# Gate and value products as three 256-column matmuls per weight tile, accumulated in one half of a PSUM bank

## The chip, the core and the metric

The kernel runs on one core of a Trainium2 chip. The metric is the time of one execution on the device, in microseconds (us). The kernel before the change takes 951.92 us (the median of two runs, 951.59 and 952.25 us).

A core has engines that run side by side. TensorE (PE in the profile) multiplies matrices. It holds one operand, the weights, in its array and streams the other through it, and it writes sums into PSUM. The profile keeps the loading of weights apart, as PEld. VectorE (DVE) and ScalarE (ACT) do elementwise work, GpSimd (POOL) and SyncE (SP) mostly issue transfers. SBUF is the working memory with 128 partitions. PSUM has eight banks of 512 fp32 numbers in each partition.

## The reference

One encoder layer for 256 positions and a width of 2048, in fp32: a norm, one input projection, windowed attention and a Fourier mix, an output projection with a residual, and then a feed-forward block, which is what the change touches:

```python
up = h @ w_up                                  # (256 x 2048) @ (2048 x 11008)
gate, val = up[..., :D_FF], up[..., D_FF:]     # D_FF = 5504
gate = conv(gate, dw_w) + dw_b                 # width 3, along the positions, per channel
act = gelu(gate) * val
x = x + act @ w_down                           # (256 x 5504) @ (5504 x 2048)
```

The result is normed once more and returned.

## The kernel before

**Products in two parts.** TensorE multiplies fp32 numbers in a rounded form here (type `float32r`), which alone is not exact enough. So each operand is split into a high part, rounded to that type, and a low part, which is what the rounding left over. A product is high times high, plus high times low, plus low times high. For a weight tile, `split_parts` does this: a ScalarE copy makes the high part `hi` (line 170), a VectorE subtraction the low part `lo` (line 171). Both lie in one buffer `parts` of 2 x 2048 + 128 numbers per partition, of which there are three in turn. `parts_tile` sets how far each part is moved inside its buffer. The table `PLACES` has these offsets, in numbers of 4 bytes: (0, 16) for "still" weights, (28, 28) for the blocks of the down-projection.

**A gate or value unit.** The up-projection is cut into 43 tiles of 128 gate channels and 43 of 128 value channels. Each of these 86 units takes a weight block of 1 MB, 128 columns of `w_up` in 16 k tiles of 128 rows. In `still_weights` the weights are what stands in the array. The moving operand is the normed input, which was put into the tiles `hT` (named hU for this stage) with the high part of the 256 positions in columns 0 to 255 and their low part in columns 256 to 511. For each k tile there are two matmuls:

```python
nc.tensor.matmul(ps, hi[:, s], h, ...)                       # line 326, 512 columns
nc.tensor.matmul(ps[:, 0:S], lo[:, s], h[:, 0:S], ...)       # line 328, 256 columns
```

The first fills a whole PSUM bank: hi times high on the left, hi times low on the right. The second adds lo times high on the left. The two halves have to be added afterwards. `scaled_sum` does that: ScalarE copies the right half to SBUF (line 810), VectorE adds the left half to it (line 812), and VectorE multiplies the sum with the norm's scale `r2b` (line 813). Then `gate_conv` and `gate_gelu`, or `val_mult`, make the activations.

**Order of the work.** The program order on each engine is written by hand. `items` is the list of all units: 16 gate and value units, then four groups in which the remaining ones alternate with products of the down-projection (`by_parts`, lines 1019 to 1021, all matmuls of 512 columns), then the last gate and value units among the last parts of the down-projection (`moving_weights`, lines 309 to 311). `ff_step(n)` runs after the matmuls of item n: it first issues what was noted under `beside` for this item (`scaled_sum` of the item before, and the convolution of the one before that), then splits the weights of item n + 2 (`split_item`), and then what was noted under `behind`. SyncE loads a raw weight block three units ahead (`load`). The first two units of the stage (gate and value of tile 0) are run together, because the last quarter of their moving operand comes late. The third one keeps its low parts back by four k tiles (`lag=4`).

The same `still_weights` makes the queries and keys earlier on, with a lag of four in each of 16 units. There the last five low parts stand one behind the other. Three small stages work with matmuls of 256 columns alone and have the same three products of parts: `fourier_rows` (line 491), `scores` (line 602) and `values` (line 674).

Of the kernel before, what the change touches and what calls it, by code (L numbers as in the profile page):

```python
# [8 lines left out]
F32 = mybir.dt.float32  # L9
F32R = mybir.dt.float32r  # L10
AF = mybir.ActivationFunctionType
ALU = mybir.AluOpType

P = 128
D = 2048
S = 256
NK = D // P
# [46 lines left out]
def ff_items():  # L64


    def ups(tiles):
        return [(kind, j) for j in tiles for kind in ("gate", "val")]

    items = ups(range(8))  # L70
    for g in range(N_GROUPS):
        todo = {
            "u": ups(range(8 * g + 8, 8 * g + 16)),
            "s": [("product", g, c, p) for c in range(2) for p in PRODUCTS[c]],
        }
        items += [todo[c].pop(0) for c in PATTERN]
        assert not any(todo.values())
    items += [("down", 0, c) for c in range(4)] + ups(LAST)
    items += [("down", 1, c) for c in range(4)] + [("last", c) for c in range(4)]
    return items  # L80
# [3 lines left out]
def block_kernel(  # L84
# [18 lines left out]
    nc = tc.nc  # L103
# [10 lines left out]
    def bank(pool, name):  # L114
        return pool.tile([P, 512], F32, tag=pool.name, name=name)


    units = [(w_in[i], 2048, "first" if i < N_QK else "still") for i in range(24)]
    units += [(w_out[i], 2048, "moving") for i in range(16)]
    n_front = len(units)  # L120
    items, up_index = ff_items(), {}
    for n, it in enumerate(items):
        if it[0] == "product":
            continue
        up_index[n] = len(units)
        if it[0] in ("gate", "val"):
            units.append((w_up[2 * it[1] + (it[0] == "val")], 2048, "still"))
        elif it[0] == "down":
            units.append((w_down_late[4 * it[1] + it[2]], 2048, "moving"))
        else:  # L130
            units.append((w_down_last[it[1]], 512 * len(LAST), "moving"))
    RAW = 3
    raws, halves = {}, {}


    PLACES = {"still": (0, 16), "first": (16, 16), "moving": (0, 0), "product": (28, 28)}

    def parts_tile(name, place):
        t = wp.tile([P, 2 * 2048 + 128], F32R, tag="parts", name=name, bufs=3)
        oh, ol = PLACES[place]  # L140
        return t[:, oh : oh + 2048], t[:, 2048 + ol : 4096 + ol]

    def load(i, pieces=1):
        if i < len(units) and i not in raws:
# [37 lines left out]
    hT = []  # L182
# [70 lines left out]
    ps = bank(dn, "ps_warm")  # L253
# [61 lines left out]
    def still_weights(hi, lo, ps, kk, lag=0):  # L315


        todo = [("hi", k) for k in kk[: lag + 1]]
        for n, k in enumerate(kk):
            todo.append(("lo", k))  # L320
            todo += [("hi", q) for q in kk[lag + 1 + n : lag + 2 + n]]
        for part, k in todo:
            h = hT[k // 4][:, k % 4, :]
            s = slice(k * P, (k + 1) * P)
            if part == "hi":
                nc.tensor.matmul(ps, hi[:, s], h, start=k == 0, stop=False)  # L326
            else:
                nc.tensor.matmul(  # L328
                    ps[:, 0:S], lo[:, s], h[:, 0:S], start=False, stop=k == NK - 1
                )  # L330

    def hk(k):
# [15 lines left out]
    before, beside, behind = {}, {}, {}  # L348

    def at(when, i, f, *a):  # L350
        when.setdefault(i, []).append((f, a))
# [13 lines left out]
    for c in range(4):  # L365
        t = base.tile([P, 4, 512], F32R, tag=f"hT{c}", name=f"hT{c}")
        hT.append(t)
    ps_u = [bank(mm, f"ps_u{b}") for b in range(2)]
    for k in range(NK):
# [5 lines left out]
        hi, lo = halves[c]  # L375
# [392 lines left out]
    for n, (c, kq) in enumerate(OUT_ORDER):  # L768
# [15 lines left out]
        if kq >= 2:  # L784
            part = "a" if kq == 2 else "f"
            ps = ps_a[c] if kq < 3 else ps_a[c, "f"]
# [15 lines left out]
    fp = ctx.enter_context(tc.tile_pool(name="fp", bufs=2))  # L802
    hT[:] = hT2
    r2b = fp.tile([P, S], F32, tag="r2b", name="r2b", bufs=1)
    parts = {}
    gate_out, sums_of, act = {}, {}, {}

    def scaled_sum(ps, name):
        tmp = fp.tile([P, S], F32, tag="ftmp", name=f"ft_{name}")
        nc.scalar.activation(tmp, ps[:, S : 2 * S], AF.Copy)  # L810
        add = fp.tile([P, S], F32, tag="fadd", name=f"fa_{name}", bufs=3)
        nc.vector.tensor_tensor(add, ps[:, 0:S], tmp, ALU.add)
        nc.vector.tensor_tensor(add, add, r2b, ALU.mult)
        sums_of[name] = add
# [85 lines left out]
    def ring_load():  # L900
        if ring_next[0] < len(ring):
            key = ring[ring_next[0]]
            ring_next[0] += 1
            ring_tiles[key] = fp.tile([P, 2048], F32, tag="rawd", name="rawd%d%d%s" % key)
            nc.sync.dma_start(ring_tiles[key], weights_of(*key))
# [20 lines left out]
    def first_sums(g, c):  # L926

        a, b = ring_tiles[g, c, "a"], ring_tiles[g, c, "b"]
        x = ring_tiles["x"] = fp.tile([P, 2048], F32, tag="sumw", name=f"sumw{g}{c}", bufs=1)
        nc.vector.tensor_tensor(x, a, b, ALU.add)  # L930
        nc.gpsimd.dma_start(b, weights_of(g, c, "d"), accum_op=ALU.add)
# [14 lines left out]
    def ff_step(n):  # L946
        todo, later[:] = list(later), []
        for f in todo:
            next(f, None)
        run(beside, n)  # L950
        split_item(n + 2)
        for f in todo:
            for _ in f:
                pass
        run(behind, n)

    def up_posts(n, kind, j, ps):
        if kind == "gate":
            at(beside, n + 1, scaled_sum, ps, f"g{j}")
            at(beside, n + 2, gate_conv, j)  # L960
            at(behind, n + 2, gate_gelu, j)
        else:
            at(beside, n + 1, scaled_sum, ps, f"v{j}")
            at(beside, n + 2, val_mult, j)
            if j % 8 == 7 and j < 8 * N_GROUPS:
                g = j // 8
                at(behind, n + 1, operand, g, "P1")
                at(behind, n + 2, operand, g, "N4")
                at(behind, n + 3, operand_sums, g, 0)
                at(behind, n + 4, operand, g, "P7")  # L970
                at(behind, n + 4, operand, g, "P2")
                at(behind, n + 5, operand_sums, g, 1)
                at(behind, n + 5, operand, g, "N5")
                at(behind, n + 6, operand, g, "N3")
                at(behind, n + 7, operand, g, "P6")
            if j >= 8 * N_GROUPS:
                at(behind, n + 2, act_parts, j)
# [37 lines left out]
    def by_parts(ps, o, hi, lo, first, last):  # L1015

        for p in range(4):
            s = slice(p * 512, (p + 1) * 512)
            nc.tensor.matmul(ps, o[:, 0, p, :], hi[:, s], start=first and p == 0, stop=False)  # L1019
            nc.tensor.matmul(ps, o[:, 1, p, :], hi[:, s], start=False, stop=False)  # L1020
            nc.tensor.matmul(ps, o[:, 0, p, :], lo[:, s], start=False, stop=last and p == 3)  # L1021
# [58 lines left out]
    for q in range(2):  # L1080
        kind, j = items[q]
        ps = bank(mm, f"ps_{kind}{j}")
# [10 lines left out]
    spread(rstd_of(tot2, D, "2"), r2b, "2")  # L1093
    ff_step(1)
    up_posts(1, *items[0], pair[0][0])
    up_posts(2, *items[1], pair[1][0])

    for n, it in enumerate(items):
        if n < 2:
            continue  # L1100
        if it[0] == "last":
            break
        if n in (8, 9):
            ring_load()
        if n == 13:
            pending.append(lambda: first_sums(0, 0))
        if it[0] in ("gate", "val"):
            kind, j = it
            ps = bank(mm, f"ps_{kind}{j}")
            still_weights(*halves.pop(up_index[n]), ps, range(NK), lag=4 if n == 2 else 0)  # L1110
            ff_step(n)
            up_posts(n, kind, j, ps)
            continue
        if it[0] == "product":
            kind, g, c, p = it
            end = g == N_GROUPS - 1
            if (c, p) in held:
                by_parts(held[c, p], parts[p], *halves.pop(it), g == 0, end)
            else:
                ps = bank(mm, f"ps_{p}{g}{c}")  # L1120
                by_parts(ps, parts[p], *halves.pop(it), True, True)
                at(beside, n + 1, product_out, g, c, p, ps)
            if end and p == "N4":
                at(behind, n + 1, shared_out, c)
        else:
            kind, g, c = it
            hi, lo = halves.pop(up_index[n])
            ps = [bank(mm, f"ps_l{g}{c}{b}") for b in range(2)]
            for b in range(2):
                moving_weights(hi, lo, 512, LATE[g], act.get, b, ps[b], True, True)  # L1130
            at(beside, n + 1, down_out, c, ps)
            if (g, c) == (0, 0):
                gfb = fp.tile([P, D], F32, tag="sumw", name="gfb", bufs=1)
                nc.gpsimd.dma_start(gfb, normf_g.partition_broadcast(P))
        ff_step(n)
# [149 lines left out]
```

## Time and profile before

| | |
|---|---|
| median of the runs | 951.92 us |
| the profiled execution | 953.02 us |
| its span in the profile | 951.2 us |
| TensorE matmuls | 5089, busy 940.7 us |
| weight loads | 5089, busy 813.0 us |
| VectorE | busy 744.8 us |
| ScalarE | busy 540.3 us |

The span runs from the first to the last instruction, and some 1.8 us of the execution lie around it. The time of one matmul in the profile is longer than its distance to the next, because the next one starts while the one before still drains. So the distances from start to start, which the view of instructions in order of time gives, say what a matmul costs, and not its own duration. The duration of a weight load is to be read in the same way.

### The profile page before, as it was taken

How to read it: one execution, taken by the hardware profiler on the slowest of the kernel's cores; microseconds unless marked ns; L12 is line 12 of the kernel's file. 1: busy time of each engine (PE TensorE's matmuls, PEld its weight loads, DVE VectorE, ACT ScalarE, POOL GpSimd, SP SyncE). 2: the span in 40 equal slices, each digit the busy share in tenths (PEclk: the TensorE clock that was granted, in tenths of full speed). 3: DMA queues.
4: the chain of work that ended last, by engine and by line, in shares of the span. 5: the costliest groups of instructions: out<-in, count | busy, mean ns of one | idle time of the engine just before them, and what ended most of it. 6: DMA issues, size and time to landing. Idle time of an engine off the chain costs nothing.

```text
span 951.2 us, 12801 instructions
## 1 busy us (share of the span) xinstructions
PE 940.7 (99%) x5089; PEld 813.0 (85%) x5089; DVE 744.8 (78%) x924; ACT 540.3 (57%) x654; POOL 44.7 (5%) x59
## 2 busy tenths in 40 slices
PE   8999999999999999999999999999999999999996
PEld 7788999888888888888888888888888888888885
DVE  5667878667676779887898877998889979888774
ACT  5846666544464456655555555565556755653444
POOL 0000000000000000000000000000000000000003
PEclk9999999999999999999999999999999999999999
DMA  8844444445556675978687787777987696765542
GB/s 313 346 180 178 147 164 140 171 177 177 183 177 216 265 240 202 260 254 282 214 271 232 239 291 257 251 238 223 295 253 245 213 294 201 243 241 205 197 133 89
DMA packets 33548, 211.59 MB, mean 222 GB/s; under 512 B 3792, under 2 KB 4304, under 8 KB 9424
## 3 DMA queue, kind: packets, MB, share of 16 engines
q1 hardware_dynamic: 29744, 184.54, 52.1%
q0 software_dynamic: 3600, 26.22, 14.2%
q8 instruction: 40, 0.66, 0.2%
q14 instruction: 20, 0.16, 0.1%
q10 hardware_dynamic: 144, 0.01, 0.0%
HBM read 208.65 MB, written 2.10 MB: 222 GB/s over the span
## 4 chain that ended last, share of the span: by engine, by line
PE 92%; DVE 3%; DMA 2%; issue 1%; ACT 1%; SPq 0%; POOL 0%; ACTq 0%; POOLq 0%
PE ps_val L326 16%; PE ps_gate L326 16%; PE ps_val L328 8%; PE ps_gate L328 8%; PE ps_q L326 5%; PE ps_P L1020 3%; PE ps_P L1021 3%; PE ps_P L1019 3%; PE ps_q L328 2%; PE ps_a L311 2%; PE ps_a L309 2%; PE ps_a L310 2%; PE ps_N L1021 2%; PE ps_N L1020 2%; PE ps_N L1019 2%; DMA raw<-in_w_in 2%
## 5 line engine op out<-in xcount | busy, mean ns | idle before, releaser
L171 DVE TENSOR_TENSOR parts<-raw,parts 128x2048 fp32r<-128x2048 f32 (+3 forms) x145 | 313.1, 2159 | 62.5 <-ACT parts L170 62.5
L170 ACT ACTIVATE parts<-raw 128x2048 fp32r<-128x2048 f32 (+3 forms) x144 | 262.0, 1820 | 72.4 <-PE ps_l L311 25.9
L326 PE MATMUL ps_val<-hU,parts 128*128 128x512 f32 x688 | 236.2, 389 | 0.0
L326 PE MATMUL ps_gate<-hU,parts 128*128 128x512 f32 x688 | 235.8, 389 | 0.0
L328 PE MATMUL ps_val<-hU,parts 128*128 128x256 f32 x688 | 189.9, 276 | 0.0
L328 PE MATMUL ps_gate<-hU,parts 128*128 128x256 f32 x688 | 189.3, 276 | 0.0
L326 PEld LDWEIGHTS ps_val<-hU,parts 128*128 128x128 f32 x688 | 129.2, 188 | 26.6
L326 PEld LDWEIGHTS ps_gate<-hU,parts 128*128 128x128 f32 x688 | 129.1, 188 | 26.7
L328 PEld LDWEIGHTS ps_val<-hU,parts 128*128 128x128 f32 x688 | 129.2, 188 | 1.2 <-DVE parts L171 0.2
L328 PEld LDWEIGHTS ps_gate<-hU,parts 128*128 128x128 f32 x688 | 128.9, 188 | 1.2
L810 ACT ACTIVATE ft_g<-ps_gate 128x256 f32<-128x256 f32 x43 | 16.5, 384 | 116.6 <-PE ps_gate L328 116.6
L810 ACT ACTIVATE ft_v<-ps_val 128x256 f32<-128x256 f32 x43 | 16.5, 384 | 88.3 <-PE ps_val L328 88.3
L326 PE MATMUL ps_q<-hT,parts 128*128 128x512 f32 x192 | 61.3, 393 | 0.0
L1019 PE MATMUL ps_P<-parts_P,op_P 128*128 128x512 f32 x128 | 49.8, 389 | 0.0
L1020 PE MATMUL ps_P<-parts_P,op_P 128*128 128x512 f32 x128 | 49.8, 389 | 0.0
L1021 PE MATMUL ps_P<-parts_P,op_P 128*128 128x512 f32 x128 | 49.8, 389 | 0.0
L328 PE MATMUL ps_q<-hT,parts 128*128 128x256 f32 x192 | 45.5, 278 | 0.0
L916 DVE TENSOR_TENSOR parts_N<-sumw,parts_N 128x2048 fp32r<-128x2048 f32 x16 | 36.6, 2290 | 10.1 <-ACT parts_N L915 10.1
L326 PEld LDWEIGHTS ps_q<-hT,parts 128*128 128x128 f32 x192 | 35.2, 188 | 6.8
L309 PE MATMUL ps_a<-parts,cat 128*128 128x512 f32 x96 | 37.9, 394 | 0.0
L1021 PE MATMUL ps_N<-parts_N,op_N 128*128 128x512 f32 x96 | 37.5, 390 | 0.1
L311 PE MATMUL ps_a<-parts,cat 128*128 128x512 f32 x96 | 37.5, 390 | 0.0
(323 smaller groups left out, 1564.7 us busy)
## 6 DMA issues: line engine op xcount, KB each, us to landing
raw<-in_w_up SPq DMA_DIRECT2D x86, 1024.0 KB, 5.0
raw<-in_w_in SPq DMA_DIRECT2D x21, 1024.0 KB, 4.9
raw<-in_w_out SPq DMA_DIRECT2D x16, 1024.0 KB, 4.8
sumw<-in_w_down POOLq DMA_DIRECT2D x16, 1024.0 KB, 8.4
raw<-in_w_down_late SPq DMA_DIRECT2D x8, 1024.0 KB, 4.8
raw<-in_w_down_last SPq DMA_DIRECT2D x4, 768.0 KB, 4.2
raw<-in_w_in SPq DMA_DIRECT2D x8, 256.0 KB, 6.5
xs<-in_x SPq DMA_DIRECT2D x4, 512.0 KB, 11.1
```

Of the source, the lines that this page charges most:

```text
L170: nc.scalar.activation(hi[:, s], raw[:, s], AF.Copy)
L171: nc.vector.tensor_tensor(lo[:, s], raw[:, s], f32(hi[:, s]), ALU.subtract)
L309: nc.tensor.matmul(ps, ah, wh, start=first and q == q0, stop=False)
L310: nc.tensor.matmul(ps, al, wh, start=False, stop=False)
L311: nc.tensor.matmul(ps, ah, wl, start=False, stop=last and q == q0 + len(kk) - 1)
L326: nc.tensor.matmul(ps, hi[:, s], h, start=k == 0, stop=False)
L328: nc.tensor.matmul(ps[:, 0:S], lo[:, s], h[:, 0:S], start=False, stop=k == NK - 1)
L810: nc.scalar.activation(tmp, ps[:, S : 2 * S], AF.Copy)
L916: nc.vector.tensor_tensor(lo, src, f32(hi), ALU.subtract)
L1019: nc.tensor.matmul(ps, o[:, 0, p, :], hi[:, s], start=first and p == 0, stop=False)
L1020: nc.tensor.matmul(ps, o[:, 1, p, :], hi[:, s], start=False, stop=False)
L1021: nc.tensor.matmul(ps, o[:, 0, p, :], lo[:, s], start=False, stop=last and p == 3)
```

## The change

All gate and value units but the first two, 84 of 86, use a new function `still_thirds` in the place of `still_weights`. It issues three matmuls of 256 columns for each k tile, all of which accumulate into the left half of the bank. For 32 of the 84 units (`apart`) the product with `lo` stands between the two with `hi`. The lag of the third unit is gone. `scaled_sum` then has nothing to add: VectorE multiplies the left half with `r2b` straight out of PSUM, and the copy and the addition are left out. The 84 units also differ in the places of their parts: the first 64 of them go twice through 8 offsets of `hi` and 4 of `lo`, the last 20 have a pair each from a list, and where the offset of `hi` is the larger one, `lo` is put into the first half of the buffer and `hi` into the second.

```diff
-            units.append((w_up[2 * it[1] + (it[0] == "val")], 2048, "still"))
+            units.append((w_up[2 * it[1] + (it[0] == "val")], 2048, "up"))
...
+    def up_place():
+        n = used[0]
+        used[0] += 1
+        if n < 2:
+            return PLACES["still"]
+        n -= 2
+        if n < 64:
+            return 8 * (n % 8), 16 * (n // 8 % 4)
+        n -= 64
+        odd = [(52, 52), (52, 16), (4, 4), (20, 20), (36, 36), (60, 60), (12, 12), (28, 28),
+               (44, 44), (4, 20), (20, 52), (52, 36), (52, 0), (60, 16), (12, 16), (0, 52),
+               (16, 52), (32, 52), (48, 52), (44, 16)]
+        return odd[n]
...
-        oh, ol = PLACES[place]
-        return t[:, oh : oh + 2048], t[:, 2048 + ol : 4096 + ol]
+        oh, ol = up_place() if place == "up" else PLACES[place]
+        if oh <= ol:
+            return t[:, oh : oh + 2048], t[:, 2048 + ol : 4096 + ol]
+        return t[:, 2048 + oh : 4096 + oh], t[:, ol : ol + 2048]
...
+    def still_thirds(hi, lo, ps, apart):
+        for k in range(NK):
+            h = hT[k // 4][:, k % 4, :]
+            s = slice(k * P, (k + 1) * P)
+            todo = [(hi, 0), (hi, S), (lo, 0)]
+            if apart:
+                todo = [(hi, 0), (lo, 0), (hi, S)]
+            for n, (w, o) in enumerate(todo):
+                nc.tensor.matmul(
+                    ps[:, 0:S], w[:, s], h[:, o : o + S],
+                    start=k == 0 and n == 0, stop=k == NK - 1 and n == 2,
+                )
...
-    def scaled_sum(ps, name):
+    def scaled_sum(ps, name, whole=True):
+        if whole:
+            add = fp.tile([P, S], F32, tag="fadd", name=f"fa_{name}", bufs=3)
+            nc.vector.tensor_tensor(add, ps[:, 0:S], r2b, ALU.mult)
+            sums_of[name] = add
+            return
...
-            at(beside, n + 1, scaled_sum, ps, f"g{j}")
+            at(beside, n + 1, scaled_sum, ps, f"g{j}", j > 0)
...
-            still_weights(*halves.pop(up_index[n]), ps, range(NK), lag=4 if n == 2 else 0)
+            still_thirds(*halves.pop(up_index[n]), ps, 4 <= up_index[n] // 8 - n_front // 8 < 8)
```

More of the change, by code (lines that the diff above doesn't have):

```diff
@@ L136, in block_kernel @@
     PLACES = {"still": (0, 16), "first": (16, 16), "moving": (0, 0), "product": (28, 28)}
+    used = [0]
+    def up_place():
[11 more added lines that the diff above has]
+        return odd[n]
     def parts_tile(name, place):
         t = wp.tile([P, 2 * 2048 + 128], F32R, tag="parts", name=name, bufs=3)
-        oh, ol = PLACES[place]
-        return t[:, oh : oh + 2048], t[:, 2048 + ol : 4096 + ol]
+        oh, ol = up_place() if place == "up" else PLACES[place]
+        if oh <= ol:
+            return t[:, oh : oh + 2048], t[:, 2048 + ol : 4096 + ol]
+        return t[:, 2048 + oh : 4096 + oh], t[:, ol : ol + 2048]
     def load(i, pieces=1):
@@ L962, in up_posts @@
         else:
-            at(beside, n + 1, scaled_sum, ps, f"v{j}")
+            at(beside, n + 1, scaled_sum, ps, f"v{j}", j > 0)
             at(beside, n + 2, val_mult, j)
```

## The prediction

> **What bounds the kernel now.** I read the page's head first, then the chain that ended last, then the waits of TensorE, and last the gate and value units in order of time.
>
> ```profile
> span 951.2 us, 12801 instructions
> PE 940.7 (99%) x5089; PEld 813.0 (85%) x5089; DVE 744.8 (78%) x924; ACT 540.3 (57%) x654; POOL 44.7 (5%) x59
> PEclk9999999999999999999999999999999999999999
> ...
> PE 92%; DVE 3%; DMA 2%; issue 1%; ACT 1%; SPq 0%; POOL 0%; ACTq 0%; POOLq 0%
> PE ps_val L326 16%; PE ps_gate L326 16%; PE ps_val L328 8%; PE ps_gate L328 8%; PE ps_q L326 5%; PE ps_P L1020 3%; PE ps_P L1021 3%; PE ps_P L1019 3%; PE ps_q L328 2%; PE ps_a L311 2%; PE ps_a L309 2%; PE ps_a L310 2%; PE ps_N L1021 2%; PE ps_N L1020 2%; PE ps_N L1019 2%; DMA raw<-in_w_in 2%
> ```
>
> 92% of the chain lies on TensorE, and 48% of it in the two lines that the change rewrites. The granted clock is full throughout. So what counts is the distance between one matmul and the next. The waits of weight loads from 272 us to the end, the part that the change touches, leave almost nothing else:
>
> ```profile
> PEld ps_l L309 <- issue: 0.6, 1, 0.6
> PEld ps_N L1021 <- DVE parts_N L916: 0.5, 1, 0.5
> PEld ps_val L328 <- DVE parts L171: 0.2, 1, 0.2
> ```
>
> That is 1.3 us in all. A helper engine that gets faster can give back no more than this.
>
> **The unit as it is.** In order of time, within a gate unit, and the first matmul of a gate unit and of the value unit behind it:
>
> ```profile
> 502.14 0.28 PE L328 MATMUL ps_gate<-hU,parts 128*128 128x256 f32 x1
> 502.25 0.39 PE L326 MATMUL ps_gate<-hU,parts 128*128 128x512 f32 x1
> 502.48 0.28 PE L328 MATMUL ps_gate<-hU,parts 128*128 128x256 f32 x1
> 502.59 0.39 PE L326 MATMUL ps_gate<-hU,parts 128*128 128x512 f32 x1
> ...
> 894.21 0.39 PE L326 MATMUL ps_gate<-hU,parts 128*128 128x512 f32 x1
> ...
> 899.65 0.39 PE L326 MATMUL ps_val<-hU,parts 128*128 128x512 f32 x1
> ```
>
> From start to start the 512-column matmul takes 0.23 us and the 256-column one 0.11. A whole unit takes 899.65 - 894.21 = 5.44 us, so a k tile takes 5.44 / 16 = 0.340 us. The two shapes stand as 2 to 1, so 256 columns cost 0.340 / 3 = 0.113 us here. The streaming rate is therefore the same in both shapes: three matmuls of 256 columns at this rate take 0.340 us again. Nothing is won on TensorE; the question is whether the rate holds.
>
> **What the change does to TensorE.** A k tile gets a third weight load. In the unit as it is, each 256-column matmul, during which the next weights have to come in, is followed by one that lasts twice as long and leaves slack. Afterwards every load has only the time of a 256-column matmul. The trace has stretches of just this kind: `fourier_rows` (one long stretch, here as a piece of the chain), `values` with the same order of high, high, low, and the five low parts at the end of a query unit, each with the start of what follows.
>
> ```profile
> 49.01 2.88 PE ps_f L491 x24
> ...
> 81.71 0.76 PE L328 MATMUL ps_q<-hT,parts 128*128 128x256 f32 x5
> 82.31 0.88 PE L602 MATMUL ps_s<-kT,qT 128*128 128x256 f32 x6
> ...
> 102.25 0.40 PE L674 MATMUL ps_o<-pt,v_hi 128*128 128x256 f32 x2
> 102.48 0.28 PE L674 MATMUL ps_o<-pt,v_lo 128*128 128x256 f32 x1
> 102.60 0.40 PE L674 MATMUL ps_o<-pt,v_hi 128*128 128x256 f32 x2
> 102.84 0.28 PE L674 MATMUL ps_o<-pt,v_lo 128*128 128x256 f32 x1
> 102.96 0.60 PE L652 MATMUL ps_t<-ident,sc 128*128 128x128 f32 x4
> ```
>
> The long stretch takes 2.88 / 24 = 0.120 us per matmul. The five low parts take (82.31 - 81.71) / 5 = 0.120, and the six of `values` (102.96 - 102.25) / 6 = 0.118. None of them reaches 0.113, although their tiles lie in quite different places. The short stretches start with slack from the 512-column matmuls ahead, so the long one is nearest to a unit of 48 matmuls. I take 0.1195 us: nearer to 0.120, with a little taken off because the 84 units have many different places and some may be kinder.
>
> The two `hi` products of a k tile use the same weights, back to back in 52 units. If the second load were left out, two loads per k tile would remain. `values` answers that, since it uses `v_hi` twice running:
>
> ```profile
> L674 PEld LDWEIGHTS ps_o<-pt,v_hi x48: 187/188/192, 95.0 to 191.8; 128*128 128x128 f32 x48
> L674 PE MATMUL ps_o<-pt,v_hi x48: 278/281/285, 95.2 to 191.9; 128*128 128x256 f32 x48
> ```
>
> 48 matmuls with `v_hi`, 48 loads: the same weights are loaded again.
>
> So a k tile takes 3 x 0.1195 = 0.3585 us, 0.0185 more than now. The change covers 84 units x 16 = 1344 k tiles: **+24.9 us**. The order in the 32 units that are `apart` changes neither the number of loads nor the shapes, and I cost it at nothing.
>
> **What it does to VectorE and ScalarE.**
>
> ```profile
> L810 ACT ACTIVATE ft_v<-ps_val 128x256 f32<-128x256 f32 x43 | 16.5, 384 | 88.3 <-PE ps_val L328 88.3
> L812 DVE TENSOR_TENSOR fa_g<-ps_gate,ft_g 128x256 f32<-128x256 f32 x43 | 18.1, 422 | 24.1 <-ACT ft_g L810 24.1
> L813 DVE TENSOR_TENSOR fa_v<-fa_v,r2b 128x256 f32<-128x256 f32 x43 | 18.3, 425 | 1.5
> L915 ACT ACTIVATE parts_N<-sumw 128x2048 fp32r<-128x2048 f32 x16 | 30.6, 1910 | 0.0
> L916 DVE TENSOR_TENSOR parts_N<-sumw,parts_N 128x2048 fp32r<-128x2048 f32 x16 | 36.6, 2290 | 10.1 <-ACT parts_N L915 10.1
> L170 ACT ACTIVATE parts<-raw 128x2048 fp32r<-128x2048 f32 x130 | 248.9, 1915 | 58.7 <-PE ps_l L311 16.8 <-PE ps_a L311 14.2 <-PE ps_ff L311 9.2
> L171 DVE TENSOR_TENSOR parts<-raw,parts 128x2048 fp32r<-128x2048 f32 x130 | 297.4, 2288 | 55.5 <-ACT parts L170 55.5
> ```
>
> 84 copies of 0.384 us go from ScalarE (32 us) and 84 additions of 0.422 us from VectorE (35 us). The multiplication that stays reads PSUM as the addition did, at 0.42 us. All of it runs beside TensorE, which waits 1.3 us for everything together, so I count half of that, **-0.6 us**, as a guess between 0 and -1.3. The new wait, of VectorE for the last matmul of a unit, replaces ScalarE's wait for the same matmul and VectorE's for the copy; behind it in VectorE's queue stands the split of a unit two items ahead, as before, and it now starts earlier by a copy and an addition. The new places cost the two engines nothing that a row shows: the blocks at (28, 28) take 1910 and 2290 ns, those at the other places 1915 and 2288. The dropped lag costs nothing either: the low part of the third unit is written by 265.2 us, and its matmuls start at 272.96:
>
> ```profile
> 262.94 2.29 DVE L171 TENSOR_TENSOR parts<-raw,parts 128x2048 fp32r<-128x2048 f32 x1 [1.20 <-ACT parts L170]
> ...
> 272.96 1.40 PE L326 MATMUL ps_gate<-hU,parts 128*128 128x512 f32 x5
> ```
>
> Transfers keep their number and order on the queues of SP and POOL, and a slower TensorE only gives them more time.
>
> **The sum.** +24.9 - 0.6 = +24.3 us on the profiled execution's 953.0 us gives 977.3. That execution lies 1.1 us above the median of 951.92, so the median should become **976 us**. About 2% of the time, 19 us, is what a measurement of this kernel can tell from no change.
>
> **Rivals.**
>
> *The loads stay hidden (not slower).* The rate of 0.113 us per 256 columns holds in the new units too. For it speaks that a load does fit into 0.113 us in every unit now: at 502.14 the weights of the matmul at 502.25 had to come in while 256 columns streamed. Eight transposes of 128 columns, each with a load, took even less, (265.68 - 264.89) / 8 = 0.10 us:
>
> ```profile
> 264.89 1.04 PE L750 MATMUL ps_x<-ident,xs 128*128 128x128 f32 x8
> 265.68 0.47 PE L326 MATMUL ps_val<-hU,parts 128*128 128x512 f32 x1
> ```
>
> Then the 0.120 of the stretches would come from the places of their tiles, and the places of the 84 units would mostly be kinder. The time would be 951.9 - 0.6 = 951 us, and up to 956 where the mean is 0.1145 (1344 x 0.0035 = 4.7 us more). The forecast gives way to it from a mean of 0.118 downwards: (0.118 x 3 - 0.340) x 1344 = 18.8 us, where the 2% end. Against it speak the three stretches above, none below 0.118. The Trainium skill's page "TensorE: Matmul & The Clock Gate" stands on this rival's side: its section "Back-to-back issue gap" gives N / 2.4 + 2.5 ns from one matmul to the next, and its section "LDWEIGHTS (loading the stationary operand)" gives the number of columns / 1.2 ns for a load. By these, 256 columns take an estimated 109 ns, a load 107 ns and hides, and three thirds (327 ns) against 216 + 109 = 325 ns would cost 1344 x 2 ns = 3 us. The trace does not agree with the page here: 113 and 227 ns in the alternating unit, 120 ns in the long stretch.
>
> *Bad places.* Where the weights lie sets how a load and the stream disturb each other. The same code with the same offsets already shows two rates, here at the start of a query unit's and a later unit's steady part:
>
> ```profile
> 71.34 0.40 PE L326 MATMUL ps_q<-hT,parts 128*128 128x512 f32 x1
> ...
> 74.84 0.40 PE L326 MATMUL ps_q<-hT,parts 128*128 128x512 f32 x1
> ...
> 78.09 0.39 PE L326 MATMUL ps_q<-hT,parts 128*128 128x512 f32 x1
> ...
> 81.49 0.39 PE L326 MATMUL ps_q<-hT,parts 128*128 128x512 f32 x1
> ```
>
> Ten k tiles take 3.50 us in the first and 3.40 in the second, 0.010 us more for each tile, or 0.005 for each load. If most of the new places add that to 0.120, a matmul takes 0.125, a k tile 0.375, and the time rises by 0.035 x 1344 = 47 us to 998 us. Against it: the stretches with other tiles do not come out above 0.120.
>
> *Faster.* A rate below 0.113 per 256 columns would be needed; 19 us are 0.014 us per k tile, that is 0.1085 per matmul. No place in the trace shows 256 columns in less than 0.11.
>
> **Chances.** The forecast, 0.117 to 0.123 us per matmul (+14.8 to +39.0 us, or 966 to 990 us with the 0.6 taken off): 0.70, of which 0.12 lies under the 2%. Hidden loads: 0.17. Bad places: 0.10. Faster: 0.03. That makes slower by over 2% 0.58 + 0.10 = 0.68, within 2% 0.12 + 0.17 = 0.29, faster 0.03. The range runs from 953 us, which takes in the upper half of the hidden loads, to 990 us; it leaves out 0.03, some 0.08 of the hidden loads and 0.07 of the bad places.
>
> **What the profile afterwards would show.** Matmuls should number 5089 + 1344 = 6433, with as many loads. Within a new unit the starts should lie 0.12 us apart and a unit should take 16 x 0.3585 = 5.74 us where it took 5.44, with no engine named as the cause. The groups of line 810 should shrink to two instructions, VectorE should fall by about 35 us and ScalarE by about 32. I would be wrong if the starts lie 0.113 us apart, if units with different places differ by far more than 0.1 us, or if TensorE now waits for a named engine.

## The result and the profile after

The changed kernel takes 975.18 us (median of two runs, 974.71 and 975.65) against 951.92: a ratio of 1.0244, with a 95% interval of 1.0200 to 1.0288. It is slower by 23.3 us.

The head of the page after, its chain, and the new groups (line, engine, operation, tiles, count, then busy time, mean duration in ns, and idle time of the engine before them):

```profile
span 972.6 us, 15315 instructions
PE 962.3 (99%) x6433; PEld 884.6 (91%) x6433; DVE 710.6 (73%) x840; ACT 517.1 (53%) x570; POOL 44.6 (5%) x59
...
PE 94%; DMA 3%; ACT 1%; DVE 0%; issue 0%; POOL 0%; ACTq 0%; POOLq 0%; SPq 0%
...
L360 PEld LDWEIGHTS ps_val<-hU,parts 128*128 128x128 f32 x2016 | 243.8, 188 | 2.4
L360 PE MATMUL ps_val<-hU,parts 128*128 128x256 f32 x2016 | 245.8, 281 | 0.0
L360 PEld LDWEIGHTS ps_gate<-hU,parts 128*128 128x128 f32 x2016 | 242.2, 188 | 2.4
L360 PE MATMUL ps_gate<-hU,parts 128*128 128x256 f32 x2016 | 244.1, 280 | 0.0
...
L844 DVE TENSOR_TENSOR fa_g<-ps_gate,r2b 128x256 f32<-128x256 f32 x42 | 17.7, 422 | 26.7 <-PE ps_gate L360 26.6
```

There are 1344 more matmuls and as many more loads, one for each k tile. TensorE carries 94% of the chain. VectorE is busy 34.2 us less and ScalarE 23.2 us less. Of the waits of weight loads from 272 us to the end, one is left in the place of three:

```profile
PEld ps_l L327 <- issue: 0.3, 1, 0.3
```

So the time did not go to a wait. It went to the distance between matmuls, and the units in order of time show something that no group does (start, duration, instruction; a unit lasts until the next one starts, and the last line of each piece is cut off by the end of the stretch that was asked for):

```profile
295.83 5.61 PE L360 MATMUL ps_gate<-hU,parts 128*128 128x256 f32 x48
301.28 5.82 PE L360 MATMUL ps_val<-hU,parts 128*128 128x256 f32 x48
306.94 5.71 PE L360 MATMUL ps_gate<-hU,parts 128*128 128x256 f32 x48
312.48 5.82 PE L360 MATMUL ps_val<-hU,parts 128*128 128x256 f32 x48
318.14 5.81 PE L360 MATMUL ps_gate<-hU,parts 128*128 128x256 f32 x48
323.79 5.81 PE L360 MATMUL ps_val<-hU,parts 128*128 128x256 f32 x48
329.44 5.91 PE L360 MATMUL ps_gate<-hU,parts 128*128 128x256 f32 x48
335.19 0.99 PE L360 MATMUL ps_val<-hU,parts 128*128 128x256 f32 x7
...
487.04 6.11 PE L360 MATMUL ps_val<-hU,parts 128*128 128x256 f32 x48
492.99 0.40 PE L360 MATMUL ps_gate<-hU,parts 128*128 128x256 f32 x2
```

The same 48 matmuls take 301.28 - 295.83 = 5.45 us in the first unit, whose parts lie at (32, 0), 5.66 in the next, at (40, 0), 335.19 - 329.44 = 5.75 at (16, 16) and 492.99 - 487.04 = 5.95 at (56, 48). The first is within 0.01 us of a unit before the change (5.44).

Added up from the starts of all instructions in the two traces, the 84 units take 19.3 us more than 84 x 5.44, and the matmuls of the blocks of the down-projection between them (`by_parts`) take 2.0 us more (154.7 against 152.7). The two spans differ by 21.4 us. So nearly all of the loss lies inside the units. Only 4 of the 84, at (32, 0) twice, (0, 32) and (32, 32), stay under 5.5 us.

### The profile page after: what moved, and what is told of

Read it like the earlier page. It is cut to its first block, busy times and chain, and to the rows that moved or that the text cites. A ratio compares the mean times of both kernels' runs of the same rounds, so it can differ in the third digit from the quotient of the medians.

```text
span 972.6 us, 15315 instructions
## 1 busy us (share of the span) xinstructions
PE 962.3 (99%) x6433; PEld 884.6 (91%) x6433; DVE 710.6 (73%) x840; ACT 517.1 (53%) x570; POOL 44.6 (5%) x59
## 4 chain that ended last, share of the span: by engine, by line
PE 94%; DMA 3%; ACT 1%; DVE 0%; issue 0%; POOL 0%; ACTq 0%; POOLq 0%; SPq 0%
PE ps_val L360 25%; PE ps_gate L360 24%; PE ps_q L344 5%; PE ps_P L1057 3%; PE ps_P L1059 3%; PE ps_P L1058 3%; DMA raw<-in_w_in 3%; PE ps_N L1058 2%; PE ps_q L346 2%; PE ps_N L1057 2%; PE ps_N L1059 2%; PE ps_a L329 2%; PE ps_a L327 2%; PE ps_a L328 2%; PE ps_l L327 2%; PE ps_k L344 2%
## 5 line engine op out<-in xcount | busy, mean ns | idle before, releaser
L360 PEld LDWEIGHTS ps_val<-hU,parts 128*128 128x128 f32 x2016 | 243.8, 188 | 2.4
L360 PE MATMUL ps_val<-hU,parts 128*128 128x256 f32 x2016 | 245.8, 281 | 0.0
L360 PEld LDWEIGHTS ps_gate<-hU,parts 128*128 128x128 f32 x2016 | 242.2, 188 | 2.4
L360 PE MATMUL ps_gate<-hU,parts 128*128 128x256 f32 x2016 | 244.1, 280 | 0.0
L953 ACT ACTIVATE parts_N<-sumw 128x2048 fp32r<-128x2048 f32 x16 | 30.7, 1918 | 40.0 <-PE ps_val L360 25.7
L344 PEld LDWEIGHTS ps_q<-hT,parts 128*128 128x128 f32 x192 | 35.2, 188 | 6.8
L327 PE MATMUL ps_a<-parts,cat 128*128 128x512 f32 x96 | 37.9, 394 | 0.0
L1058 PE MATMUL ps_N<-parts_N,op_N 128*128 128x512 f32 x96 | 37.7, 393 | 0.0
L1057 PE MATMUL ps_N<-parts_N,op_N 128*128 128x512 f32 x96 | 37.7, 392 | 0.0
L1059 PE MATMUL ps_N<-parts_N,op_N 128*128 128x512 f32 x96 | 37.5, 391 | 0.0
L329 PE MATMUL ps_a<-parts,cat 128*128 128x512 f32 x96 | 37.5, 390 | 0.0
L328 PE MATMUL ps_a<-parts,cat 128*128 128x512 f32 x96 | 37.4, 389 | 0.0
L844 DVE TENSOR_TENSOR fa_g<-ps_gate,r2b 128x256 f32<-128x256 f32 x42 | 17.7, 422 | 26.7 <-PE ps_gate L360 26.6
L346 PEld LDWEIGHTS ps_q<-hT,parts 128*128 128x128 f32 x192 | 33.5, 188 | 1.0
```

What stands on the lines that cost most here:

```text
L327: nc.tensor.matmul(ps, ah, wh, start=first and q == q0, stop=False)
L328: nc.tensor.matmul(ps, al, wh, start=False, stop=False)
L329: nc.tensor.matmul(ps, ah, wl, start=False, stop=last and q == q0 + len(kk) - 1)
L346: nc.tensor.matmul(ps[:, 0:S], lo[:, s], h[:, 0:S], start=False, stop=k == NK - 1)
L360: nc.tensor.matmul(ps[:, 0:S], w[:, s], h[:, o : o + S], start=k == 0 and n == 0, stop=k == NK - 1 and n == 2,)
```

## The experiments

Theory A is that of the prediction: a matmul of 256 columns with its own load needs about 0.12 us wherever things lie, because the loads pace the stream. Theory B: load and stream disturb each other, depending on where the weights lie in memory against the input that streams. Each experiment starts from the changed kernel. A unit's time is the distance between the starts of two units in the trace.

**All units at (32, 0), and all at (16, 16).**

```diff
 def up_place():
+        if n >= 2:
+            return (32, 0)        # the other run: (16, 16)
...
-    still_thirds(..., 4 <= up_index[n] // 8 - n_front // 8 < 8)
+    still_thirds(..., False)
```

> All 84 units at the place (32, 0), order hi, hi, lo, nothing else changed against the changed kernel. Theory A (the loads pace: a matmul of 256 columns with a load of its own needs about 0.12 us wherever the parts lie; the two units at this place in the changed kernel were an accident of their neighbours): units of about 5.7 us, a time of 972 to 978 us. Theory B (the place decides whether load and stream disturb each other; the two units at (32, 0) took 5.45 us, as the old form did): all units at about 5.45 us, a time of 951 to 954 us, no different from before within 0.3%.

> All 84 units at the place (16, 16), order hi, hi, lo. Theory A: as the changed kernel, 974 to 977 us. Theory B: the two units at this place took 5.75 us with a steady 0.120 per matmul; 84 x (5.75 - 5.44) = 26 us over before and about 1 to 2 us for the products between them: 978 to 981 us.

At (32, 0): 954.02 us against 951.94 for the kernel before on the same chip, a ratio of 1.0021 (1.0012 to 1.0031). At (16, 16): 979.34 us, 1.0290 (1.0273 to 1.0307). The chains of the two, in the same stretch:

```profile
305.13 5.44 PE ps_gate L362 x48
310.57 5.44 PE ps_val L362 x48
```

```profile
301.85 5.76 PE ps_val L362 x48
307.61 5.76 PE ps_gate L362 x48
```

The same program, with the parts moved by some numbers, differs by 25 us. Theory A falls: 48 matmuls with 48 loads run at 5.44 / 48 = 0.113 us each where they lie well, the rate of streaming that the prediction named as the floor. At (16, 16) each one takes 0.120, which is just what the prediction had read off the long stretch of the trace before.

**The old form with the new places.**

```diff
-            at(beside, n + 1, scaled_sum, ps, f"g{j}", j > 0)
+            at(beside, n + 1, scaled_sum, ps, f"g{j}", False)
...
-            at(beside, n + 1, scaled_sum, ps, f"v{j}", j > 0)
+            at(beside, n + 1, scaled_sum, ps, f"v{j}", False)
...
-            still_thirds(*halves.pop(up_index[n]), ps, 4 <= up_index[n] // 8 - n_front // 8 < 8)
+            still_weights(*halves.pop(up_index[n]), ps, range(NK), lag=4 if n == 2 else 0)
```

> The old form of a unit (512 and 256 columns, copy and addition of halves) with the 84 places of the changed kernel. Theory A: a load has slack in the long matmul, so the places do not matter: 951 to 953 us, every unit 5.44 us. Theory B: the places disturb here too, but with two loads for a k tile instead of three and slack behind one of them, so less: units between 5.44 and about 5.65 us that differ by place, 954 to 963 us.

967.12 us against 951.94, 1.0157 (1.0137 to 1.0177), which is more than either theory gave. The places alone, with two matmuls for a k tile as before, cost 15 us. Units go from 5.44 us, at (0, 16), (0, 52) and (32, 52), up to 5.66, and most lie at 5.55 to 5.65. (The first one takes 5.72; it is slower than the others in the kernel before too, with 5.57.) The long matmuls are not spared: at other places those of 512 columns took 228 to 235 ns on average in most units, where they had taken 227.

**The input moved.** In the built program the tiles of the input start 24 numbers behind a multiple of 32, and the buffers of the weight parts 8. So at (32, 0) both weight parts lie 16 from the input, counted in lines of 32 numbers, and at (16, 16) they lie at 0. Here 16 numbers stand ahead of the input's tiles and 48 behind them, so that the input alone moves by 16.

```diff
+    pad = base.tile([P, 16], F32, tag="pad0", name="pad0")
+    nc.gpsimd.memset(pad, 0.0)
     for c in range(4):
         t = base.tile([P, 4, 512], F32R, tag=f"hT{c}", name=f"hT{c}")
         hT.append(t)
+    pad = base.tile([P, 48], F32, tag="pad1", name="pad1")
+    nc.gpsimd.memset(pad, 0.0)
```

> The changed kernel with the moving operand's four tiles 16 numbers further on; the weight parts stay where they were against a line of 64 numbers. Theory A: nothing changes, each unit as in the changed kernel. Theory B, with the distance between weights and stream as what counts: the good places move by 16, so that (16, 48), (48, 16), (48, 48) or (16, 16) have units of 5.44 us, and (32, 0), (0, 32) and (32, 32) lose theirs and go to 5.65 to 5.75. Theory C (the place of the weights alone counts): the good places stay at (32, 0), (0, 32), (32, 32). The total says little here: 965 to 982 us by all of them.

977.74 us (1.0269, 1.0248 to 1.0289), which says little, as expected. The units say much. Here are those at (16, 16), (24, 16), (32, 16), (40, 16) and (48, 16), and the start of the next one:

```profile
332.45 5.81 PE L360 MATMUL ps_gate<-hU,parts 128*128 128x256 f32 x48
338.10 5.86 PE L360 MATMUL ps_val<-hU,parts 128*128 128x256 f32 x48
343.80 5.82 PE L360 MATMUL ps_gate<-hU,parts 128*128 128x256 f32 x48
349.46 5.83 PE L360 MATMUL ps_val<-hU,parts 128*128 128x256 f32 x48
355.12 5.61 PE L360 MATMUL ps_gate<-hU,parts 128*128 128x256 f32 x48
360.57 5.82 PE L360 MATMUL ps_val<-hU,parts 128*128 128x256 f32 x48
```

From start to start the one at (16, 16) takes 5.65 us and the one at (48, 16) 360.57 - 355.12 = 5.45; they had taken 5.75 and 5.70. Each of these places was used once in the order high, high, low and once in the order high, low, high. The two times of each kernel, in us, are those of the two orders, first high, high, low:

```
place       changed kernel    input moved by 16
(32, 0)     5.45  5.45        5.72  5.71
(0, 32)     5.44  5.71        5.67  5.69
(32, 32)    5.44  5.65        5.74  5.76
(16, 16)    5.75  5.75        5.65  5.65
(48, 16)    5.70  5.68        5.45  5.46
(16, 48)    5.71  5.72        5.47  5.70
(48, 48)    5.70  5.70        5.65  5.44
(0, 0)      5.74  5.65        5.84  5.69
(56, 48)    5.94  5.95        5.71  5.72
(8, 0)      5.66  5.65        5.95  5.92
```

The table turns over. What was best at (32, 0) is now best at (48, 16), and what was worst at (56, 48) is now worst at (8, 0), which is (56, 48) moved by 16, counted in lines of 64. The whole grid moves so: of 62 pairs of units in the same order whose two offsets differ by 16 (without the first unit of the stage), 50 agree within 0.03 us, while units at unchanged offsets agree in 21 of 62. What counts is the distance between weights and stream and not the place of the weights alone, which was theory C. That two units at one place can differ by 0.2 us is taken up below.

One pair does not fit a rule in lines of 32. At (0, 0) both parts lie 16 from the input too, and with the input moved they do so at (16, 16). None of these four units is fast (5.74 and 5.65, 5.65 and 5.65; the first of them is the first unit of the stage). So 16 in lines of 32 names the good places found here, but it is not shown to be enough.

**The new form alone, at the place of before.** All units at (0, 16), in the order high, high, low.

> The new form alone: all 84 units with three thirds, order hi, hi, lo, all at (0, 16), the place that every unit had before. Theory B (the distance of each weight part from the stream, taken in lines of 32 numbers, decides; hi is at a good distance there and lo at the bad one): the two units at this place took 5.65 us in the changed kernel, so 84 x 0.21 = 17.8 us and 1 to 2 us beside: 969 to 973 us. Theory E (the cost of the change lies in the new places alone, and the old one is good for both forms): 952 to 955 us.

970.44 us against 952.04, 1.0195 (1.0179 to 1.0210), and the units take 5.65 us in the chain:

```profile
301.02 5.65 PE ps_val L362 x48
306.67 5.65 PE ps_gate L362 x48
312.33 5.65 PE ps_val L362 x48
```

So the place at which the old form runs at its floor costs the new form 18 us. Each form has its own good places. The new places alone cost 15 us and the new form alone 18, but both together 23: the two costs do not add up.

**The saved work put back.** All units at (32, 0), and in `scaled_sum`:

```diff
+            tmp = fp.tile([P, S], F32, tag="ftmp", name=f"ft_{name}")
+            nc.scalar.activation(tmp, ps[:, 0:S], AF.Copy, scale=0.0)
+            nc.vector.tensor_tensor(add, ps[:, 0:S], tmp, ALU.add)
-            nc.vector.tensor_tensor(add, ps[:, 0:S], r2b, ALU.mult)
+            nc.vector.tensor_tensor(add, add, r2b, ALU.mult)
```

> As the run with all units at (32, 0), but with ScalarE's copy (of the left half, times zero) and VectorE's addition kept in every unit, so that both have the work of before again. If that work was hidden: 953 to 955 us, as without it. If the work taken off ScalarE and VectorE gives anything back: over 955 us.

954.24 us, 1.0021 (1.0011 to 1.0030), where it was 954.02 and 1.0021 without that work. The copies and additions were hidden: taking them away gives nothing that can be measured.

**All units at (32, 32).**

> All 84 units at (32, 32), order hi, hi, lo. In the changed kernel one unit at this place took 5.44 us in the order hi, hi, lo and one 5.65 in the order hi, lo, hi. Theory F (at a good distance two steady rhythms are possible, and how a unit is entered decides which it keeps): units of both kinds in one order, 955 to 970 us, and the slow ones steady at 118, 118, 117 ns. Theory G (the order of the products decides): all at 5.44, 952 to 955 us. Theory H (which of the three buffers a unit has decides): the slow ones come at every third buffer.

970.63 us, 1.0191 (1.0171 to 1.0211). The chain shows one place and one order with two speeds:

```profile
356.00 5.44 PE ps_val L362 x48
361.44 5.44 PE ps_gate L362 x48
369.60 5.65 PE ps_val L362 x48
378.03 5.65 PE ps_gate L362 x48
```

The 16 units after the first, which still has to settle, take 5.44 us. Then the first block of the down-projection comes in, and every unit from there to the end takes 5.65 to 5.66, steady at 118, 118, 117 ns. The order of the products does not do this, since it is the same on either side, and neither do the three buffers, which take turns on either side: theory F. The rhythm lasts: even a unit that follows another one without a block between them stays at 5.65.

**The same with the blocks of the down-projection moved.** The first load of a unit runs beside the last matmul of the block ahead of it: in the trace of this run, the first load behind the first block starts at 367.96 us, together with that matmul.

```diff
-    PLACES = {... "product": (28, 28)}
+    PLACES = {... "product": (16, 16)}
```

> All units at (32, 32), and the blocks of the down-projection at (16, 16) in the place of (28, 28). At (32, 32) the first 17 units kept 5.44 us, and every unit behind a block of the down-projection took 5.65. The first load of a unit runs beside the last product of that block; with the block at (16, 16) it lies 16 numbers from the stream, the good distance, where it was 4. Theory F1 (the disturbance of this one first load sets the rhythm of the unit): the units behind products go back to 5.44 us, and the time falls by 10 us or more, unless the products themselves become slower at their new place. Theory F2 (any change of the matmuls' length throws the rhythm): they stay at 5.65, 968 to 973 us.

956.11 us against 952.44, 1.0035 (1.0015 to 1.0054), 14.5 us less than with the blocks at (28, 28). The units behind blocks are fast again:

```profile
354.73 5.44 PE ps_val L362 x48
360.17 5.44 PE ps_gate L362 x48
368.35 5.45 PE ps_val L362 x48
376.55 5.45 PE ps_gate L362 x48
```

Nothing in the units was changed. Of the 14.5 us, 12.4 lie in the units and 1.3 in the blocks themselves. So what stands ahead of a unit can set the speed of all its 48 matmuls, and theory F2 falls. The last six units say the same from the other side. They stand behind the last parts of the down-projection (`moving_weights`), which were not moved, and there the slow rhythm is back:

```profile
873.97 5.66 PE ps_gate L362 x48
879.62 5.65 PE ps_val L362 x48
```

That it is the first load alone, as theory F1 says, is not shown. The move also changed the distance inside a block, between its own weights and what it streams, from 4 to 16. And in the changed kernel the unit at (32, 32) that took 5.44 us stood behind a block at (28, 28) as well, at the same distance as the slow ones here. The rhythm in which the block itself was left may have a part in it. What stands ahead is the likely reason why units at one place differ in the changed kernel too. The order of the products alone is not: with the input moved, at (48, 48), it is the unit in the other order that is fast.

**The load by itself.** Each matmul of 256 columns, but the first and the last of a unit, is cut into two of 128, each with its own load:

```diff
+                ends = (k == 0 and n == 0) or (k == NK - 1 and n == 2)
+                width = S if ends else P
+                for q in range(0, S, width):
+                    nc.tensor.matmul(ps[:, q : q + width], w[:, s], h[:, o + q : o + q + width], ...)
```

> All units at (32, 0) with each matmul of 256 columns cut into two of 128 (but the first and the last of a unit), each with its own load, so that the load alone sets the distance and can be read. If a load needs about 0.120 us by itself (theory A): 0.120 per matmul, units of about 11.5 us, some 1460 us in all. If it needs 0.107 to 0.110 and the rest was disturbance (theory B): units of about 10.3 to 10.6 us, 1355 to 1385 us.

> The cut into matmuls of 128 columns, as in the run before with all units at (32, 0), now at (16, 16). At (32, 0) the distance was 0.111 us on average and a unit 10.51 us. If a stream at the bad distance delays the load: 0.115 to 0.125 us, units of 10.9 to 11.9 us. If it is the stream that is delayed by the load, it has slack here, and the distance stays at 0.111: 10.5 us.

1381.24 us at (32, 0) and 1380.52 at (16, 16), one run each. Here the chain of the second one; the units of the first also take 10.51:

```profile
304.24 10.51 PE ps_val L365 x94
314.75 10.51 PE ps_gate L365 x94
325.27 10.51 PE ps_val L365 x94
```

A matmul comes every 10.51 / 94 = 0.112 us on average in both. So a load fits into the 0.113 us of 256 columns, and a bad distance does not slow the loads where the stream has slack. That speaks for the stream as the one that gives way. It does not show it: with 128 columns the two meet in another rhythm.

**The other order at (32, 0).** `still_thirds(..., True)`, all in the order high, low, high.

> All units at (32, 0), all in the order hi, lo, hi. The order has no part in it where no load is disturbed: 953 to 955 us, units of 5.44 to 5.46, as in the order hi, hi, lo. If the order counts: another time by more than 2 us.

956.11 us against 952.44, 1.0034 (1.0020 to 1.0048), a little over what was expected. The units behind a block take 5.48 us where they took 5.45 in the other order: they need about three k tiles until they run at 0.113, where the other order needs one. The order counts for 1 to 2 us here.

**What stays open.** At its best place the new form is still 2.1 us slower than the kernel before. The trace shows 0.8 us of that in the units and 0.35 in what follows the last matmul, and another 0.3 lies outside the span (the profiled execution is 953.32 us and its span 951.2, where it was 953.02 and 951.2). The rest, well under 1 us, can't be placed, since the part ahead of the stage alone differs by 0.8 us between the two traces. Nor did any run show why 16 numbers are a good distance, why (0, 0) is not a good place, or why the old form wants another pair: at (0, 16) its high part lies 16 from the input, and its low part at 0. In lines of 32 that is so at (32, 16) too, where the old form took 5.60 and 5.65 us.

## Why the prediction was right, and where it was not

*The bound.* Right. TensorE's distances set the time, and the chain after is 94% TensorE.

*The same streaming rate in both shapes.* Right: 0.113 us per 256 columns is the floor of the new form too, reached with all units at (32, 0).

*A third load for each k tile, also for repeated weights.* Right: 6433 loads, 1344 more.

*0.1195 us per matmul, +24.9 us.* The number was nearly right and its reason wrong. The 84 units average 0.118 us (84 x 5.44 + 19.3 = 476.3 us, over 84 x 48 matmuls). The prediction took the 0.118 to 0.120 us of the stretches before for the price of a load. The runs show the price of a distance instead: with the parts at a good one a matmul with its load takes 0.113, no more than its streaming, and with a bad one, as at (16, 16), 0.120. The step that failed is the sentence that none of the stretches reaches 0.113 "although their tiles lie in quite different places". Three stretches were taken for proof that the place does not matter, and in the built program none of them lies at the good distance. The five low parts of a query unit stand at an offset of 16, which is 0 from the input, as in the run with all units at (16, 16). The operands of `values` lie 0 apart as well, and those of `fourier_rows` 8, all in lines of 32. No run moved these stretches themselves.

That the total came out is in part luck. The 84 places are a sample of distances with nearly the mean of the three stretches, and other differences made up for the rest: the units cost 19.3 us and not 24.9, the blocks between them 2.0 and not nothing, and from median to median the time rose by 23.3 us where it rose by 21.7 between the two profiled executions. The prediction had named a sign of being wrong, "units with different places differ by far more than 0.1 us". It came: they differ by up to 0.5 us.

*The rival of the hidden loads* got 0.17, with the condition that the places be kind. Where they are, its 951 to 956 us came out (954.02). The condition was what should have been priced: 4 of the 84 units had it. The row that bore it out stood in the trace, the load within 0.113 us in every unit. The other row that was brought for it is misread: the eight transposes start 0.109 us apart and not 0.10, since what follows the last of them starts only 0.028 us behind it. The page "TensorE: Matmul & The Clock Gate" of the Trainium skill gives P / 1.2 ns for the load of P columns (section "LDWEIGHTS (loading the stationary operand)"), which is an estimated 107 ns for 128. The runs with 128 columns agree within 5%, at 112.

*Bad places* was the right mechanism with too small a part. The prediction had it add 0.005 us to 0.120 in the worst case. In truth the places range from 0.113 to 0.124 (5.95 / 48), and the 0.120 was inside this range and not its start. The two rates that it read off two query units, 3.50 and 3.40 us for ten k tiles at the same offsets, can't come from the place alone; they look like the two rhythms at (32, 32). The same page of the Trainium skill says, in the section "Step-by-step: what each phase is for", that loading the next weights does not steal read bandwidth from the matmul that runs, since the two have separate ports. The runs do not bear that out as a rule about time: 5.44 against 5.76 us for the same instructions. Whether it is read bandwidth that is lost, no run shows.

*The order of the products at nothing.* Nearly right at (32, 0), where it is worth 1 to 2 us. At other places it was not run by itself.

*VectorE and ScalarE.* The 35 us on VectorE came out (34.2). ScalarE lost 23.2 and not 32: in the trace before, a copy of 0.384 us overlaps the instruction behind it by 0.10 us on average, so that a removed one frees less than its duration. The -0.6 us did not come: the waits did fall, from 1.3 to 0.3 us, but putting the work back changed nothing.

*What was missed.* The blocks of the down-projection became 2.0 us slower, though not an instruction of theirs was changed. A likely reason is that they are entered in another rhythm, as the units behind them are; no run shows it by itself.

## What to carry to other kernels

Where weight loads and matmuls follow each other without slack, the offset between the two operands in memory is a tuning knob of its own, worth 6% of such a stretch here (5.44 against 5.76 us). A form of the loop can't be judged before each candidate has been tried at its own good offsets: at one set of offsets the old form won by 18 us, at the best of each the two differ by 2. And a rate that a trace shows in a few stretches is a floor only if the thing that may set it was varied there, and the offsets in the built program show whether it was.

## What the runs showed of the hardware

- The same 48 matmuls with 48 loads take between 5.44 and 5.95 us, by the distance of the weights from the streamed operand, while the granted clock is full (0.998 in the two profiled runs at 951.2 and 977.1 us of span). For three thirds, the places that reached 5.44 us all have both parts 16 numbers (64 bytes) from the input in lines of 32, though (0, 0), which also has, took 5.65. A distance of 0 for both parts is bad (5.67 to 5.76 us, 0.118 to 0.120 per matmul).
- A stream of matmuls can keep its rhythm, good or bad, over many units of the same form: at (32, 32) for 16 units at 5.44 us, and behind the first foreign block at 5.65 until the end.
- What stands just ahead can set that rhythm: moving a neighbour's operand by 12 numbers was worth 14.5 us.
- With matmuls of 128 columns, each with its own load, one comes every 0.112 us, at a good distance and at a bad one.
